# Expert routing in a two-block transformer kernel: 112 candidate sums in place of 256, and the last gate block copied beside the others

## The chip, the core and the metric

The kernel runs on one core of a Trainium2 chip. The metric is the device time of one execution in microseconds (us); a lower time is better. TensorE (PE) multiplies matrices, VectorE (DVE) and ScalarE (ACT) work elementwise, GpSimd (POOL) and SyncE (SP) issue transfers here. Each engine takes its instructions in the order in which the program was built, and a framework places that order with a model of its own when the kernel is built.

## The reference

The program computes two transformer blocks for 512 tokens of 1024 features. The change lies in the last part, a layer of 16384 experts (128 x 128 key pairs) in which every token is sent to 16 experts for each of 8 heads:

```python
q = (hc @ w_query).reshape(PEER_CHUNK, PEER_HEADS, PEER_KEY_DIM)
s1 = jnp.einsum('chk,nk->chn', q[..., :PEER_HALF_DIM], keys_1)
s2 = jnp.einsum('chk,nk->chn', q[..., PEER_HALF_DIM:], keys_2)
v1, i1 = lax.top_k(s1, 16)
v2, i2 = lax.top_k(s2, 16)
cand = (v1[..., :, None] + v2[..., None, :]).reshape(PEER_CHUNK, PEER_HEADS, -1)
cand_idx = (i1[..., :, None] * N_KEYS + i2[..., None, :]).reshape(...)
top_s, pos = lax.top_k(cand, 16)
experts = jnp.take_along_axis(cand_idx, pos, axis=-1)
gate = jax.nn.softmax(top_s)
act = jax.nn.gelu(jnp.einsum('chkd,cd->chk', jnp.take(expert_u, experts, axis=0), hc))
out = jnp.einsum('chkd,chk->cd', jnp.take(expert_v, experts, axis=0), gate * act)
```

Of the 256 sums of two sorted lists of 16, the pair (i, j), counted from zero, has (i+1)(j+1)-1 sums that are no smaller, so it can be among the best 16 only if (i+1)(j+1) is at most 16.

## The kernel before

The first 384 tokens meet all experts: `eu` holds 128 rows of weights (L1080, `run_ahead`), each one product of 24 matmuls with 384 columns on PE, then gelu on ScalarE, then a store to `spill` in memory. The last 128 tokens meet their own experts alone, whose rows are gathered by index on GpSimd's queue (L1156, `gather`), multiplied with the token and summed on VectorE (L1162, `gather_dot`; L1168, `gather_sum`).

The layer has these stages. **Routing** (L1187, `route`): eight rounds, one for each head. A round has two products of 24 matmuls with 512 columns for the query, the scores against 128 keys, `top16` (L1178) on VectorE for four token tiles and two halves, then the 256 sums `cand` (L1240) and `top16` over them for four token tiles; for token tile 3 `chosen` (L1198) turns positions into the expert numbers that the gathers of the next round use. Beside it each round runs nine experts of U and, from the second round on, 13 gathered rows. **Gates**: `chosen` for the 8 heads of the other tiles and the softmax. **Spreading** (L1272, `spread`): gates become a dense table [i2, i1, token] in blocks of 32 tokens; the first 11 blocks go through `gstage` to `gdram` in memory, the 12th stays on the chip as `glast`. **Last stage** (in `peer`): for each of 128 experts the stored activations `pact` (for the last 15, `kept`) are multiplied with the gates (L1123 for 11 blocks out of `gtile`, which is loaded for four experts at a time, L1124 for the 12th out of `glast`), split in a high and a low part (`pwh`, `pwl`), the row of V is loaded and split (`vh`, `vl`), and PE adds 24 matmuls into eight banks.

Every weight is split in two: ScalarE casts the high part (`split`, L190), VectorE subtracts the low part (L191, `wlo`), and PE's third matmul of a group needs it. The split weights have two buffers, so ScalarE's cast waits until PE has finished the product before. A shared pool `row` of five buffers holds the rows of U, of V and the gathered rows.

What sets the order: `later` (L164) gives U's matmuls a lower priority; everything else is taken by the framework in its modelled order of readiness. VectorE carries U's `wlo`, the gathered rows, and `top16` in one queue.

Of the kernel before, what the change touches and what calls it, by code (L numbers as in the profile page):

```python
# [33 lines left out]
# ---------------------------------------------------------------- host layout  # L34
# [116 lines left out]
class Builder:  # L151
# [12 lines left out]
    # the block's instructions give way to what is traced up to n instructions later  # L164
# [11 lines left out]
    # banks of the accumulator memory: six by number, two for the large products  # L176
# [6 lines left out]
    # the banks of the large products in turn: the two, and the given others while they are free  # L183
# [4 lines left out]
    # src -> hi + lo, both exact in float32r  # L188
# [13 lines left out]
    # n more buffers for the weights, or none  # L202
# [5 lines left out]
    # one [128, n] block of (x @ w).T; w in dram [128, kc, 128], x as hi / lo [128, kc, 512]  # L208
# [18 lines left out]
    # the same for several w, side by side: step blocks of x for each in turn  # L227
# [15 lines left out]
    # (ss / n + eps) ** -0.5 on a small tile  # L243
# [7 lines left out]
    # row vector over all partitions: out[p, t] = r[t % 128, t // 128]  # L251
# [6 lines left out]
    # sums of squares over the features: all blocks but the last are added up; over the partitions, token-major  # L258
# [13 lines left out]
    # 1 / rms over all partitions  # L272
# [9 lines left out]
    # h = rmsnorm(x) * sw + sh, split into hi / lo  # L282
# [15 lines left out]
    # x[m] += gate[m] * (w applied to the hi / lo source), sums of squares of the new x  # L298
# [10 lines left out]
    # 128 features of one section of silu(c) @ ada_w + ada_b, feature-major  # L309
# [19 lines left out]
    # the tiles still to do of the given sections, n at a time, behind more urgent work  # L329
# [17 lines left out]
    # sigmoid through exp  # L347
# [40 lines left out]
    # ------------------------------------------------------------ first block  # L388
    def block1(self):
        A, V, x = self.A, self.V, self.x  # L390
        with ExitStack() as st1:
# [7 lines left out]
            with ExitStack() as st2:  # L399
# [12 lines left out]
                # scale and shift of feature block k, and weights ahead of their first use  # L412
# [79 lines left out]
    # token-major part of the projection: ga, gbeta, ng, v_slc, v_win  # L492
    def proj_small(self, hi, lo):
# [7 lines left out]
        class Small:  # L501
            # the weights of the next feature blocks
# [43 lines left out]
    # depthwise causal convolution and silu of one block of the projection  # L546
# [47 lines left out]
    # decay rates, beta and the cumulated decays, token-major [128, head, token tile]  # L594
# [37 lines left out]
    # what of one head needs its keys alone: decays, the triangular inverse, w  # L632
    def gdn_inv(self, h):
# [7 lines left out]
        # f = beta / |k|^2, rn = |k|  # L641
# [26 lines left out]
        # X = (I + strictly upper Bm)^-1 by blocks of doubling size; Tm = X.T  # L668
# [27 lines left out]
        # k e^gc ; k f e^(gl - gc)  # L696
# [11 lines left out]
    # the rest of one head that does not need the state  # L708
# [17 lines left out]
    # scan over the chunks, the four heads together; output norm and gate  # L726
# [32 lines left out]
    def gdn_out(self):  # L759
# [3 lines left out]
        # rmsnorm(o) * w * silu(z); the missing |q| and dk^-0.5 go into its eps  # L763
# [15 lines left out]
    # keys and values of the three attentions; the norm weights of q go into the keys  # L779
# [58 lines left out]
    # the three attentions of one token tile; the output takes the place of q  # L838
    def nsa(self, kp, t, last):
# [7 lines left out]
        # compressed keys, four heads at once  # L847
# [90 lines left out]
    # ----------------------------------------------------------- second block  # L938
    def mixer2(self):
# [7 lines left out]
        with ExitStack() as st:  # L947
# [59 lines left out]
            # per-token sums over the 512 channels  # L1007
# [34 lines left out]
            self.update(A["wo2"], KD, mh, ml, self.mod(1, 2))  # L1042

    # The tokens up to ND meet every expert: gelu(U h), times a gate that is zero for the experts not chosen, times V.
    # The last 128 tokens meet their own experts, whose rows are gathered.
    def peer(self):
        A, V, C, x = self.A, self.V, self.C, self.x
        sw = self.scaled(1, 4, "n22")
# [281 lines left out]
```

## Time and profile before

| | |
|---|---|
| runs of the kernel before | 2490.15, 2495.16, 2498.87 us (median 2495.16) |
| the profiled execution | span 2508.0 us, 35062 instructions |
| PE busy | 2396.5 us (96%) |
| weight loads (PEld) busy | 2161.5 us (86%) |
| VectorE busy | 1848.0 us (74%) |
| ScalarE busy | 1071.4 us (43%) |
| GpSimd busy | 367.0 us (15%) |
| DMA | 509.39 MB, 203 GB/s on average |

The page gives no other time for the profiled execution than its span; it is 12.8 us above the median of the runs shown. Shares are averages over stages, so each stage is read by itself: the routing stage runs from 1157 to 1609 us of the span, gates to 1682, spreading to 1954, the last stage to 2491.

### The profile page before, as it was taken

Reading aid. Unit: us, or ns where it says so; the run is one execution under the profiler, and the core shown is the slowest. Engines: PE = TensorE matmul, PEld = TensorE weight load, DVE = VectorE, ACT = ScalarE, POOL = GpSimd, SP = SyncE. Lnnn points to the kernel's source line nnn. Section 1 sums busy time; section 2 is a strip of 40 time slices with the busy share of each in tenths; the row PEclk is TensorE's granted clock in tenths of the full one; section 3 lists DMA queues with packets and bytes.
Section 4 is the critical chain, followed back from the end, with each engine's and each line's share of the span. In section 5 each row is a group of like instructions: output and inputs, shape, how many; then the busy total and the mean of one; then the engine's idle time right before and its main releaser. Section 6 shows DMA issues by size and latency. Waiting matters only on the chain. (4 is left out here: it accounts for less than half of the span.)

```text
span 2508.0 us, 35062 instructions
## 1 busy us (share of the span) xinstructions
PE 2396.5 (96%) x12749; PEld 2161.5 (86%) x12749; DVE 1848.0 (74%) x3826; ACT 1071.4 (43%) x1751; POOL 367.0 (15%) x284
## 2 busy tenths in 40 slices
PE   8999999899999999999889998999998999999998
PEld 7788787678878777878888888999898999999997
DVE  6764634778874499657778888999886878887774
ACT  4534623343432233334222232459998433333332
POOL 0000000000000000000222222123210333334420
PEclk9999888899999999999999999999999999999998
DMA  7332102465554222243777776669885999999981
GB/s 277 126 124 68 43 9 84 165 199 190 190 182 138 78 97 90 70 151 101 241 245 253 256 231 229 220 221 323 317 294 201 326 335 344 336 348 311 347 304 59
DMA packets 197933, 509.39 MB, mean 203 GB/s; under 512 B 20352, under 2 KB 93312, under 8 KB 195840
## 3 DMA queue, kind: packets, MB, share of 16 engines
q1 hardware_dynamic: 160896, 372.92, 43.7%
q0 software_dynamic: 36864, 134.23, 15.6%
q8 instruction: 100, 1.64, 0.3%
q14 instruction: 73, 0.60, 0.1%
HBM read 459.71 MB, written 47.38 MB: 202 GB/s over the span
## 5 line engine op out<-in xcount | busy, mean ns | idle before, releaser
L162 PE MATMUL acc<-hi,wlo 128*128 128x384 f32 (+1 forms) x1488 | 544.5, 366 | 41.3 <-DVE wlo L191 40.9
L162 PE MATMUL acc<-hi,whi 128*128 128x384 f32 (+1 forms) x1488 | 541.2, 364 | 2.4 <-ACT whi L190 1.2
L162 PE MATMUL acc<-lo,whi 128*128 128x384 f32 (+1 forms) x1488 | 537.3, 361 | 0.0
L190 ACT CAST whi<-raw 128x1024 fp32r<-128x1024 f32 (+2 forms) x168 | 167.5, 999 | 443.8 <-PE p L162 234.7
L162 PEld LDWEIGHTS acc<-hi,wlo 128*128 128x128 f32 x1488 | 283.7, 191 | 77.1 <-DVE wlo L191 56.1
L162 PEld LDWEIGHTS acc<-hi,whi 128*128 128x128 f32 x1488 | 284.1, 191 | 23.9 <-ACT whi L190 2.1
L162 PEld LDWEIGHTS acc<-lo,whi 128*128 128x128 f32 x1488 | 283.9, 191 | 20.2 <-issue 1.0
L191 DVE TENSOR_TENSOR wlo<-raw,whi 128x1024 fp32r<-128x1024 f32 (+2 forms) x168 | 194.3, 1157 | 104.3 <-ACT whi L190 101.9
L190 ACT CAST whi<-row 128x1024 fp32r<-128x1024 f32 x128 | 135.1, 1055 | 307.8 <-PE acc L162 286.5
L1158 POOL DMA_INDIRECT row<-in_ev_dram,eidx x128 | 199.2, 1556 | 431.7 <-DVE vl L191 251.9
L162 PE MATMUL p<-pwl,vh 128*128 128x384 f32 x768 | 257.7, 336 | 0.9 <-DVE pwl L191 0.9
L162 PE MATMUL p<-pwh,vh 128*128 128x384 f32 x768 | 254.4, 335 | 2.6 <-ACT pwh L190 2.6
L162 PE MATMUL p<-pwh,vl 128*128 128x384 f32 x768 | 252.5, 336 | 0.0
L1158 POOL DMA_INDIRECT row<-in_er_dram,eidx x128 | 148.2, 1158 | 501.4 <-DVE row L1165 167.1
L1175 DVE SCALAR_TENSOR_TENSOR pN<-row,dots,pN 128x1024 f32<-128x1024 f32 x127 | 162.7, 1281 | 79.4 <-DMA row<-in_ev_dram,eidx 79.2
L1165 DVE SCALAR_TENSOR_TENSOR row<-row,hN 128x1024 f32<-128x1024 f32 x128 | 155.8, 1220 | 67.4 <-DMA row<-in_er_dram,eidx 66.9
L162 PE MATMUL p<-hi,whi 128*128 128x512 f32 x432 | 171.9, 404 | 8.2 <-ACT hi L292 6.4
L191 DVE TENSOR_TENSOR wlo<-row,whi 128x1024 fp32r<-128x1024 f32 x128 | 155.9, 1218 | 31.4 <-ACT whi L190 30.7
L191 DVE TENSOR_TENSOR vl<-row,vh 128x1024 fp32r<-128x1024 f32 x128 | 155.8, 1219 | 29.9 <-ACT vh L190 29.9
L190 ACT CAST vh<-row 128x1024 fp32r<-128x1024 f32 x128 | 133.8, 1051 | 97.3 <-DMA row<-in_ev_dram 51.7
L162 PE MATMUL p<-hi,wlo 128*128 128x512 f32 x432 | 173.8, 403 | 1.3 <-DVE wlo L191 1.3
L162 PE MATMUL p<-lo,whi 128*128 128x512 f32 x432 | 173.3, 401 | 1.7 <-DVE lo L293 1.7
(500 smaller groups left out, 4579.6 us busy)
## 6 DMA issues: line engine op xcount, KB each, us to landing
row<-in_eu_dram SPq DMA_DIRECT2D x128, 512.0 KB
row<-in_ev_dram SPq DMA_DIRECT2D x128, 512.0 KB
araw<-in_ada_dram SPq DMA_DIRECT2D x64, 512.0 KB
raw<-in_up_dram SPq DMA_DIRECT2D x44, 512.0 KB
gdram<-gstage SPq DMA_DIRECT2D x11, 2048.0 KB
gtile<-gdram SPq DMA_DIRECT2D x31, 704.0 KB
spill<-pact SPq DMA_DIRECT2D x113, 192.0 KB
pact<-spill SPq DMA_DIRECT2D x113, 192.0 KB
```

The costliest lines, as they stand in the source:

```text
L162: self.T.matmul(out, lhsT, rhs, start=start, stop=stop)
L190: self.C.copy(hi, src)
L191: self.V.tensor_tensor(lo, src, hi.bitcast(F32), ALU.subtract)
L1158: self.G.indirect_dma_start(out=u, out_offset=None, in_=self.A[src], in_offset=bass.IndirectOffsetOnAxis(ap=self.eidx[:, s:s + 1], axis=0))
L1165: self.V.scalar_tensor_tensor(u, u, 1.0, self.hN, ALU.mult, ALU.mult, accum_out=self.dots[:, s:s + 1])
L1175: self.V.scalar_tensor_tensor(self.pN, v, w, self.pN, ALU.mult, ALU.add)
```

## The change

Two edits, apart from removed comments.

**Sums.** A region of 112 sums takes the place of the 256: for the first four keys of the first half all 16 of the second, for the other twelve the first four of the second half (64 + 48). All pairs with (i+1)(j+1) at most 16 lie in it. The sums are made for token tile 3 and for tiles 0 to 2 together, in two pieces each, and `top16` goes over 112 columns. Since the position in this layout no longer has the first key in its upper bits, `chosen` gets three more operations that turn it into the position of the 256 layout.

```diff
-            V.tensor_scalar(ab[:, 0], px, 4, None, ALU.logical_shift_right)
-            V.tensor_scalar(ab[:, 1], px, 15, None, ALU.bitwise_and)
+            wide = rp.tile([P, n, 16], U32, name=f"wide{n}", bufs=1)
+            V.tensor_scalar(wide, px, 124, None, ALU.bitwise_and)
+            V.tensor_scalar(wide, wide, 64, 3, ALU.max, ALU.mult)
+            V.scalar_tensor_tensor(wide, wide, 192, px, ALU.subtract, ALU.add)
+            V.tensor_scalar(ab[:, 0], wide, 4, None, ALU.logical_shift_right)
+            V.tensor_scalar(ab[:, 1], wide, 15, None, ALU.bitwise_and)
...
+            cands = {}
+            for t0, n in ((3, 1), (0, 3)):
+                cand = rp.tile([P, n, NC], F32, name=f"cand{n}", bufs=2)
+                for i0, i1, nj in ((0, 4, 16), (4, 16, 4)):
+                    b4 = [P, n, i1 - i0, nj]
+                    o = cand[:, :, 0:64] if i0 == 0 else cand[:, :, 64:NC]
...
+                    V.tensor_tensor(o, a, b, ALU.add)
+                cands.update({t0 + i: cand[:, i, :] for i in range(n)})
             for t in (3, 0, 1, 2):
-                cand = rp.tile([P, 16, 16], F32, name="cand", bufs=2)
-                b3 = [P, 16, 16]
-                V.tensor_tensor(cand, v_[:, t, h, 0, :].unsqueeze(2).to_broadcast(b3),
-                                v_[:, t, h, 1, :].unsqueeze(1).to_broadcast(b3), ALU.add)
-                self.top16(cand.rearrange("p a b -> p (a b)"), ts[:, t, h, :], px[:, t, h, :])
+                self.top16(cands[t], ts[:, t, h, :], px[:, t, h, :])
```

**Gates of the last 32 tokens.** `gtile` gets a 12th block; ScalarE copies it from `glast` for four experts at a time, and one multiplication with 384 columns takes the place of two (352 and 32).

```diff
-                            gt = wk.tile([P, NB - 1, GA, TB], F32, name="gtile", bufs=2)[:, :, :n, :]
+                            gt = wk.tile([P, NB, GA, TB], F32, name="gtile", bufs=2)[:, :, :n, :]
...
-                        self.dma(gt, gd[:, :, e:e + n, :].rearrange("b p a t -> p b a t"))
+                        self.dma(gt[:, :NB - 1], gd[:, :, e:e + n, :].rearrange("b p a t -> p b a t"))
+                        C.copy(gt[:, NB - 1], gl[:, e:e + n, :])
...
-                    V.tensor_tensor(a3[:, :NB - 1, :], a3[:, :NB - 1, :], gt[:, :, e - e0, :], ALU.mult)
-                    V.tensor_tensor(a3[:, NB - 1, :], a3[:, NB - 1, :], gl[:, e, :], ALU.mult)
+                    V.tensor_tensor(a3, a3, gt[:, :, e - e0, :], ALU.mult)
```

PE's order is the same up to the end of the routing stage; the order of VectorE changes from the first round on. VectorE in the later part of a round, before (`wlo` is the low part of a weight of U, `row,dots` a gathered row, MAX, MAX_INDEX and MATCH_REPLACE are the steps of `top16`, `px` the positions found):

```order
L191 TENSOR_TENSOR wlo<-row,whi 128x1024
L1180 MAX ts<-cand 128x8
L1181 MAX_INDEX px<-ts,cand 128x8
L1165 SCALAR_TENSOR_TENSOR row,dots<-row,hN 128x1024
L1181 MAX_INDEX px<-ts,cand 128x8
L1182 MATCH_REPLACE cand<-ts,cand 128x256
L191 TENSOR_TENSOR wlo<-row,whi 128x1024
L1165 SCALAR_TENSOR_TENSOR row,dots<-row,hN 128x1024
L1182 MATCH_REPLACE cand<-ts,cand 128x256
L1183 MAX ts<-cand 128x8
L191 TENSOR_TENSOR wlo<-row,whi 128x1024
```

The same place on VectorE after:

```order
L191 TENSOR_TENSOR wlo<-row,whi 128x1024
L1181 MAX_INDEX px<-ts,cand_10487 128x8
L1181 MAX_INDEX px<-ts,cand_10490 128x8 x3
L1165 SCALAR_TENSOR_TENSOR row,dots<-row,hN 128x1024
L1182 MATCH_REPLACE cand_10487<-ts,cand_10487 128x112
L1182 MATCH_REPLACE cand_10490<-ts,cand_10490 128x112 x3
L191 TENSOR_TENSOR wlo<-row,whi 128x1024
L1165 SCALAR_TENSOR_TENSOR row,dots<-row,hN 128x1024
L1183 MAX ts<-cand_10487 128x8
L1183 MAX ts<-cand_10490 128x8 x3
L191 TENSOR_TENSOR wlo<-row,whi 128x1024
```

All four tiles are now searched together between two low parts, where before two were under way at a time.

ScalarE in the last stage, once it runs evenly, after (`pwh` is the high part of the gated activations, `vh` that of a row of V); before, the same casts alternate with no copy among them:

```order
L190 CAST vh<-row 128x1024
L1117 COPY gtile<-glast 128x128
L190 CAST pwh<-pact 128x384
L190 CAST vh<-row 128x1024
L190 CAST pwh<-pact 128x384
L190 CAST vh<-row 128x1024
L190 CAST pwh<-pact 128x384
L190 CAST vh<-row 128x1024
L190 CAST pwh<-pact 128x384
L190 CAST vh<-row 128x1024
L1117 COPY gtile<-glast 128x128
```

One copy stands in ScalarE's queue for every four experts.

VectorE where the last stage begins, before (`hN` holds the gates of the first two experts, `pN` is the sum of the gathered rows of V); the multiplications of the fifteen `kept` activations follow one another, of which three are shown:

```order
L1123 TENSOR_TENSOR pact<-pact,hN 128x352 x2
L1175 SCALAR_TENSOR_TENSOR pN<-row,dots,pN 128x1024
L1124 TENSOR_TENSOR pact<-pact,glast 128x32 x4
L1124 TENSOR_TENSOR kept_15430<-kept_15430,glast 128x32
L1124 TENSOR_TENSOR kept_15526<-kept_15526,glast 128x32
L1124 TENSOR_TENSOR kept_15604<-kept_15604,glast 128x32
```

And after:

```order
L1124 TENSOR_TENSOR pact<-pact,hN 128x384 x2
L1175 SCALAR_TENSOR_TENSOR pN<-row,dots,pN 128x1024
L191 TENSOR_TENSOR pwl<-pact,pwh 128x384
L191 TENSOR_TENSOR vl<-row,vh 128x1024
L191 TENSOR_TENSOR pwl<-pact,pwh 128x384
L191 TENSOR_TENSOR vl<-row,vh 128x1024
```

The nineteen small multiplications in front of the first low parts are gone; PE has 41 matmuls of U left behind its last product of the spreading stage, where it had 5.

## Rows read from the trace of the kernel before

**Rows 1.** Busy time by stage; columns: window, length, then each engine, clock, DMA.

```profile
1157.33:1608.56 451.23, 415.64 (x2212) 389.66 (x2210) 374.99 (x1166) 137.01 (x195) 101.10 (x91) 0.98 0.71 235
...
1681.69:1953.54 271.85, 254.54 (x1678) 247.27 (x1678) 222.92 (x609) 259.60 (x559) 57.20 (x48) 0.99 0.79 278
1953.54:2490.93 537.39, 536.44 (x3080) 535.65 (x3080) 419.49 (x624) 193.46 (x261) 176.68 (x108) 0.99 0.88 310
```

**Rows 2.** The same view of the eight runs of expert products between queries.

```profile
1162.26:1195.96 33.70, 33.70 (x194) 33.70 (x193) 27.43 (x99) 11.01 (x17) 3.99 (x3) 1.00 0.47 155
...
1273.94:1318.23 44.29, 37.57 (x196) 36.29 (x195) 35.98 (x116) 11.37 (x17) 11.84 (x11) 0.92 0.79 255
...
sum 325.47, PE 291.39 PEld 281.59 DVE 275.75 ACT 95.68 POOL 75.41; mean PE 36.42 PEld 35.20 DVE 34.47 ACT 11.96 POOL 9.43
```

**Rows 3.** Waits in the routing stage, of PE and VectorE: total us, times, longest.

```profile
PE acc L162 <- DVE wlo L191: 35.4, 26, 4.4
...
DVE row L1165 <- DMA row<-in_er_dram,eidx: 64.8, 49, 5.0
```

**Rows 4.** VectorE in order of time, head 5, 256 sums: start us, us, instruction.

```profile
1437.33 0.74 DVE L1183 MAX8 ts<-cand 128x8 f32<-128x256 f32 x2
1437.99 0.41 DVE L1211 TENSOR_TENSOR eq<-abf,ca 128x256 f32<-128x256 f32 x1
1438.31 0.08 DVE L1184 MATCH_VALUE_LOAD px<-ts,cand 128x8 f32 x1
...
1438.72 0.07 DVE L1184 MATCH_VALUE_LOAD px<-ts,cand 128x8 f32 x1
```

**Rows 5.** The same view, searches of 128 scores.

```profile
1398.44 0.85 DVE L1180 MAX8 tv<-rsc 128x8 f32<-128x128 f32 x4
1399.21 0.07 DVE L1184 MATCH_VALUE_LOAD tix<-tv,rsc 128x8 f32 x1
...
1399.47 0.07 DVE L1184 MATCH_VALUE_LOAD tix<-tv,rsc 128x8 f32 x1
```

**Rows 6.** The same view, two dependent operations on 16 columns.

```profile
1443.79 0.17 DVE L1245 SCALAR_TENSOR_TENSOR ch<-ch 128x16 f32<-128x16 f32 x1
1443.99 0.17 DVE L1246 CAST eidx<-ch 128x16 int32<-128x16 f32 x1
```

**Rows 7.** Waits of PE from 16 us into rounds 1 and 6 on.

```profile
PE acc L162 <- DVE wlo L191: 2.5, 2, 1.3
...
PE acc L162 <- DVE wlo L191: 5.3, 3, 3.7
```

**Rows 8.** VectorE in order of time, the longest stall for a gathered row.

```profile
1304.37 1.22 DVE L1165 SCALAR_TENSOR_TENSOR row<-row,hN 128x1024 f32<-128x1024 f32 x1 [4.96 <-DMA row<-in_er_dram,eidx]
```

**Rows 9.** VectorE in order of time, last stage, one expert of V.

```profile
2305.33 0.52 DVE L1123 TENSOR_TENSOR pact<-pact,gtile 128x352 f32<-128x352 f32 x1
2305.77 0.19 DVE L1124 TENSOR_TENSOR pact<-pact,glast 128x32 f32<-128x32 f32 x1
2305.87 1.22 DVE L191 TENSOR_TENSOR vl<-row,vh 128x1024 fp32r<-128x1024 f32 x1
```

**Rows 10.** PE in order of time where the last stage begins.

```profile
1953.54 1.31 PE L162 MATMUL p<-pwh,vh 128*128 128x384 f32 x6 [2.65 <-ACT pwh L190]
...
1956.44 0.69 PE L162 MATMUL p<-pwl,vh 128*128 128x384 f32 x1 [0.94 <-DVE pwl L191]
```

**Rows 11.** ScalarE casts of gated activations, the whole program: busy us, mean ns.

```profile
L190 ACT CAST pwh<-pact 128x384 fp32r<-128x384 f32 x113 | 58.0, 514 | 226.0 <-issue 135.0 <-PE acc L162 78.3 <-DVE pwl L191 4.7
```

**Rows 12.** ScalarE, VectorE and PE, last stage, where a row of V lands late.

```profile
2308.73 1.05 ACT L190 CAST vh<-row 128x1024 fp32r<-128x1024 f32 x1 [5.20 <-DMA row<-in_ev_dram]
...
2309.94 1.22 DVE L191 TENSOR_TENSOR vl<-row,vh 128x1024 fp32r<-128x1024 f32 x1
...
2311.13 0.33 PE L162 MATMUL p<-pwh,vh 128*128 128x384 f32 x1
```

**Rows 13.** VectorE in the spreading stage: a stall for a gathered row of V.

```profile
1894.92 1.29 DVE L1175 SCALAR_TENSOR_TENSOR pN<-row,dots,pN 128x1024 f32<-128x1024 f32 x1 [9.52 <-DMA row<-in_ev_dram,eidx]
```

More of the change, by code (lines that the diff above doesn't have):

```diff
@@ L1112, in peer @@
                         if e:
-                            gt = wk.tile([P, NB - 1, GA, TB], F32, name="gtile", bufs=2)[:, :, :n, :]
+                            gt = wk.tile([P, NB, GA, TB], F32, name="gtile", bufs=2)[:, :, :n, :]
                         else:
-                            gt = self.hN[:, :(NB - 1) * n * TB].rearrange("p (b a t) -> p b a t", b=NB - 1, a=n)
-                        self.dma(gt, gd[:, :, e:e + n, :].rearrange("b p a t -> p b a t"))
+                            gt = self.hN[:, :NB * n * TB].rearrange("p (b a t) -> p b a t", b=NB, a=n)
+                        self.dma(gt[:, :NB - 1], gd[:, :, e:e + n, :].rearrange("b p a t -> p b a t"))
+                        C.copy(gt[:, NB - 1], gl[:, e:e + n, :])
                     if e < KEPT:
@@ L1195, in route @@
         self.gi = self.gs_ = 0
+        NC = 112
         def chosen(px, ix, n, out=None):
@@ L1236, in route @@
                     self.top16(sc[:, t, :], v_[:, t, h, s, :], ix[:, t, h, s, :])
-            for t in (3, 0, 1, 2):
-                cand = rp.tile([P, 16, 16], F32, name="cand", bufs=2)
-                b3 = [P, 16, 16]
-                V.tensor_tensor(cand, v_[:, t, h, 0, :].unsqueeze(2).to_broadcast(b3),
-                                v_[:, t, h, 1, :].unsqueeze(1).to_broadcast(b3), ALU.add)
-                self.top16(cand.rearrange("p a b -> p (a b)"), ts[:, t, h, :], px[:, t, h, :])
+            cands = {}
[4 more added lines that the diff above has]
+                    o = cand[:, :, 0:64] if i0 == 0 else cand[:, :, 64:NC]
+                    o = o.rearrange("p t (i j) -> p t i j", j=nj)
+                    a = v_[:, t0:t0 + n, h, 0, i0:i1].unsqueeze(3).to_broadcast(b4)
+                    b = v_[:, t0:t0 + n, h, 1, 0:nj].unsqueeze(2).to_broadcast(b4)
+                    if n == 1:
+                        o, a, b = (v.squeeze(1) if hasattr(v, "squeeze") else v[:, 0] for v in (o, a, b))
+                    V.tensor_tensor(o, a, b, ALU.add)
+                cands.update({t0 + i: cand[:, i, :] for i in range(n)})
+            for t in (3, 0, 1, 2):
+                self.top16(cands[t], ts[:, t, h, :], px[:, t, h, :])
                 if t == 3:
```

## Prediction

> **What bounds the kernel now.** I read the busy time by stage first, then the same view of pieces of one stage, then the waits, then single stretches in order of time. In the last stage PE is busy for 536.4 of 537.4 us [rows 1]: 3080 matmuls, 174.5 ns each, 4.19 us for the 24 of one expert. Nothing that VectorE saves there can shorten it. In the routing stage PE is busy for 415.6 of 451.2 us and VectorE for 375.0 [rows 1], so neither is saturated, and the reader is to see why in the runs of expert products that lie between the queries of two heads [rows 2]. In the first run no rows are gathered yet, and 191 matmuls take 33.70 us at full clock, 176.4 ns each. All eight runs hold 191 + 6 x 193 + 219 = 1568 such matmuls, which would be 276.7 us at that rate; they take 325.47 us. So 48.8 us are lost, all in runs two to eight. The third is the worst: 44.29 us for 193 matmuls (34.0 at the full rate), with a mean clock of 0.92, so part of it ran at the lower of the two levels after a long wait. The waits say who is late: PE stood 35.4 us, 26 times, for `wlo`, the low part of a weight of U on VectorE, and VectorE itself stood 64.8 us, 49 times, for gathered rows [rows 3]. VectorE is therefore late partly by its work and partly by transfers, and the question of this change is what a shorter VectorE queue does to a stage with both.
>
> **The searches.** Head 5 shows the spacing of the steps on 256 sums [rows 4]: two MAX8 from 1437.33 to 1437.99 are 0.33 each, a FIND_INDEX8 with the load in front of it 1438.72 - 1438.31 = 0.41. A search is two MAX8, two FIND_INDEX8 and one MATCH_REPLACE8, which I take like FIND_INDEX8: 0.66 + 1.23 = 1.89 us. On 128 scores [rows 5] MAX8 is (1399.21 - 1398.44) / 4 = 0.19 and FIND_INDEX8 0.26, a search 0.38 + 0.78 = 1.16. The 128 columns cost 0.73, so 144 fewer save 0.82 us, and four tiles 3.3 us per head.
>
> **The sums.** Four sums of 256 at the spacing of MAX8 are 1.32 us per head. By the same slope (1.1 ns a column on 0.05) the new pieces of 48, 64, 144 and 192 columns are 0.10, 0.12, 0.21 and 0.26, in all 0.69. That saves 0.6; the bound on the bad side, for broadcasts in four dimensions that run slower, is no saving.
>
> **The three operations more in `chosen`.** They depend on each other. Two dependent operations on 16 columns start 0.20 us apart [rows 6]; the bounds are 0.08, the length of a value load in [rows 4], and 0.20. I take 0.20, since each reads what the one before wrote: 0.6 us per head. Net 3.3 + 0.6 - 0.6 = 3.3 us per head, 26 us in eight. The three calls for all heads at once add nine operations on 128 columns, each under the 0.41 of a step on 256 [rows 4], at most 3.7 us behind the routing stage, where PE has products of U in stock; I take 1 us.
>
> **What of it reaches the end.** The first round has no loss to recover, so at most 7 x 3.3 = 23 us. Below that the saving must meet a wait. The searches over sums begin some 16 us into a run; from there to the end of the run PE waits between 2.5 and 5.3 us in each of rounds 1 to 6 (the first and the last of six answers stand in [rows 7]; they are 2.5, 4.6, 3.5, 3.7, 3.5 and 5.3), 23.1 us together. In two of them the long wait, 4.4 and 3.7 us, follows a stall of VectorE for a gathered row, the worse one of 4.96 us [rows 8]; shorter searches don't bring that row sooner. That leaves 15 us of waits that sit behind VectorE's own work. Up to 3.3 us of work less per round against waits of 2.5 on average, some of which move on to the next gathered row: I take 12 us, from bounds of 0 (the gathered rows take all) and 23.
>
> **The gates of the last 32 tokens.** For one expert the two multiplications start 0.44 us apart, and the second is followed after 0.10 [rows 9]; with 384 columns instead of 352 I expect 0.48 in place of 0.54. That is VectorE's time in a stage in which PE is never idle [rows 1]: worth nothing, covered by PE, and 8 us if that cover were gone. ScalarE gets 32 copies of at most 128 columns, each under the 0.51 us of a cast of 384 [rows 11], 16 us at most, in a stage in which it is busy for 193.5 of 537.4 us [rows 1]. At the beginning of the stage PE stood 2.65 us for the first `pwh` and 0.94 for the first `pwl` [rows 10], with nineteen small multiplications in VectorE's queue between. In the changed order they are gone and 41 products of U, some 7 us, cover the end of spreading instead of 5. But ScalarE must still take the gelu of the last expert, then cast `pwh` and `vh`, before PE goes on. I take a gain of 1 us, from bounds of 4 lost and 4 gained.
>
> **Spreading** keeps its work, but its order moves. Before, a gathered row of V held VectorE for 9.52 us [rows 13] and with it the one-hot tables that PE needs. Such a stall can vanish or come twice; I take zero, within 6 us either way.
>
> Sum: 12 - 1 + 1 = 12 us. The profiled span of 2508.0 us would become 2496; against the median of the runs, 2495.2, it is **2483 us**. What a measurement of this kernel can tell from no change is about 0.3%, 7.5 us.
>
> **Rivals.**
>
> *The gathered rows take the saving.* Five `row` buffers serve weights of U and gathered rows; VectorE reaches the next gathered row sooner and waits longer for it, so the 64.8 us of [rows 3] grow by what the searches lose. For it: in rounds with gathers VectorE stands still somewhere in every one. Against it: 15 us of PE's waits sit behind VectorE's own work. It gives 0 to 4 us, about 2493. The Trainium skill has a rule that points this way (Perfetto Trace Analysis, Optimization Strategy): the same gap repeating on the engine that should be saturated can mean that there are too few buffers for the next tile. By that rule all of PE's waits are a matter of the five buffers and the time stays; the trace bears it out in the two long waits above, and not in the others.
>
> *The saving comes through whole.* Waits of over 3 us put PE's clock down to its lower level afterwards (the 0.92 of [rows 2]); if most fall away, the clock comes back as well, and the stall of [rows 13] may go with the new order. 23 us, some 4 of clock or stall, less 1: about 2469.
>
> *The copies hold the casts up: slower.* A copy into `gtile` may not start before VectorE has read the last activation of the tile two before, and the next `pwh` and `vh` stand behind it on ScalarE; on VectorE that read is queued behind gathered rows of V. While PE has a lead of several experts this costs nothing. From about 2280 to 2430 us the lead is gone: a row of V lands 5.20 us late, its low part runs from 2309.94 to 2311.16, and PE begins that expert at 2311.13 [rows 12]. There are (2430 - 2280) / 4.19 = 36 experts and nine copies in this stretch. If each holds the casts for one expert's share of VectorE, 419.5 / 128 = 3.3 us [rows 1], that is 30 us lost against 12 gained: about 2513. It decides from the point where a copy comes free later than the next row of V lands. Against it: VectorE needs 3.3 us of the 4.19, and activations are gated well ahead of rows of V. The Trainium skill (TensorE: Matmul & The Clock Gate, Architectural detail: the array is 16x 32x32) has ScalarE and VectorE take their queues strictly in order, which this rival needs; the trace agrees, with everything behind the stall of [rows 13] waiting 9.52 us.
>
> *The new order loses elsewhere what routing gains.* A second stall like that of [rows 13], about 10 us with its slow clock, gives 2495.
>
> **How the numbers follow.** Forecast, 2476 to 2489: 0.55. Gathered rows take it, 2491 to 2497: 0.22. Whole, 2463 to 2475: 0.13. Copies, 2500 to 2515: 0.06. Lost elsewhere, 2492 to 2500: 0.04. The range that leaves out the copies and the better part of the whole saving is 2467 to 2499. Faster by over 0.3% (under 2487.7) are nine tenths of the forecast and the whole saving, 0.62; slower (over 2502.6) the copies and a little of the last case, 0.07; the rest, 0.31, is within.
>
> **What would show it.** Right: in the runs of [rows 2] the sum falls from 325 to about 313 us and PE's wait for `wlo` from 35 to about 23; searches on 112 columns last some 0.15 us less a step than on 256; VectorE's busy time in routing falls by some 26 us; the last stage still takes 24 matmuls in 4.19 us per expert. Wrong: VectorE's wait for gathered rows grows by as much as its work falls (first rival); PE waits for `vl` or `pwh` in the last third of the last stage (the copies); the spreading stage differs from 272 us by more than 6.

## The result and the profile after

The changed kernel takes **2512.6 us** (median of 10 runs), the kernel before 2498.4 us on the same chip (median of 10): a ratio of 1.0068, with a 95% interval of 1.0043 to 1.0092. It is slower by 0.7%, some 17 us by the ratio and 14 by the medians. The forecast was 2483 us, faster; the time lies above the range of 2467 to 2499.

The profiled executions have spans of 2515.6 and 2508.0 us. The part of the program ahead of routing is the same in both and happened to run 10 us shorter after: the first expert product behind the first scores starts at 1147.23 instead of 1157.33 us, and over all the kernels of this text between 1142 and 1157. So the changed part by itself is 18.5 us longer, and I compare it in two pieces. The first is routing, gates and spreading up to the first product with V, the second the last stage. Busy time by stage, first the kernel before (its last stage stands in [rows 1]):

```profile
1157.33:1953.54 796.21, 740.27 (x4282) 705.00 (x4280) 667.96 (x1849) 428.08 (x801) 170.67 (x148) 0.98 0.73 246
```

and the changed kernel:

```profile
1147.23:1954.63 807.40, 746.28 (x4282) 711.17 (x4280) 643.55 (x1873) 428.65 (x802) 175.55 (x148) 0.98 0.71 242
1954.63:2499.32 544.69, 537.51 (x3079) 535.70 (x3080) 412.02 (x503) 201.94 (x293) 178.72 (x108) 0.99 0.87 306
```

Behind the length stand the busy times of PE, of the weight loads and, third, of VectorE: 24.4 us of work less in the first piece, as forecast, and yet the piece is 11.2 us longer, 7.4 of them in routing and gates and 3.8 in spreading. The last stage is 7.3 us longer with nearly the same work for PE.

The searches cost what the forecast said. VectorE in order of time in the changed kernel, one head:

```profile
1407.79 0.80 DVE L1180 MAX8 ts<-cand 128x8 f32<-128x112 f32 x4
1408.51 1.21 DVE L191 TENSOR_TENSOR wlo<-row,whi 128x1024 fp32r<-128x1024 f32 x1
...
1409.70 0.27 DVE L1181 FIND_INDEX8 px<-ts,cand 128x8 uint32<-128x112 f32 x1
...
1409.95 0.27 DVE L1181 FIND_INDEX8 px<-ts,cand 128x8 uint32<-128x112 f32 x1
...
1424.05 0.17 DVE L1206 SCALAR_TENSOR_TENSOR wide<-wide,px 128x16 uint32<-128x16 uint32 x1
1424.25 0.17 DVE L1207 TENSOR_SCALAR ab<-wide 128x16 uint32<-128x16 uint32 x1
```

Four MAX8 fit between 1407.79 and 1408.51, 0.18 us each, where [rows 4] had 0.33; one FIND_INDEX8 starts 0.25 behind the other, where it was 0.41; a dependent operation on 16 columns takes 0.20, as in [rows 6].

The gain is missing in the eight runs of expert products (same view as [rows 2]):

```profile
1152.17:1185.87 33.70, 33.70 (x194) 33.70 (x193) 25.04 (x103) 11.03 (x17) 4.71 (x4) 1.00 0.52 173
1206.90:1250.85 43.95, 37.18 (x197) 35.89 (x196) 35.61 (x135) 11.38 (x17) 10.81 (x10) 0.92 0.71 237
...
sum 325.27, PE 286.68 PEld 279.54 DVE 271.62 ACT 94.06 POOL 74.82; mean PE 35.83 PEld 34.94 DVE 33.95 ACT 11.76 POOL 9.35
```

The sum is 325.27 us, as before, though the runs now hold 26 matmuls fewer (1542 instead of 1568). The waits show what took the place of the work. Routing and gates, total, times and longest; the kernel before:

```profile
DVE row L1165 <- DMA row<-in_er_dram,eidx: 66.9, 51, 5.0
...
PE acc L162 <- DVE wlo L191: 37.4, 29, 4.4
```

and the changed kernel:

```profile
DVE row L1165 <- DMA row<-in_er_dram,eidx: 106.3, 49, 5.6
...
PE acc L162 <- DVE wlo L191: 45.3, 24, 4.1
```

VectorE waits 39 us more for gathered rows, in as many waits: more than the 24 us of work that it lost. PE's wait for `wlo` grew by 8 us with it, where the forecast had it fall by 12.

The last stage loses 4.5 of its 7.3 us within its first 72 matmuls (view of [rows 10], with VectorE beside it):

```profile
1954.63 0.44 PE L162 MATMUL p<-pwh,vh 128*128 128x384 f32 x1 [1.92 <-ACT vh L190]
1959.24 0.69 PE L162 MATMUL p<-pwl,vh 128*128 128x384 f32 x1 [4.16 <-DVE pwl L191]
...
1957.43 1.28 DVE L1175 SCALAR_TENSOR_TENSOR pN<-row,dots,pN 128x1024 f32<-128x1024 f32 x1 [3.95 <-DMA row<-in_ev_dram,eidx]
1958.63 0.55 DVE L191 TENSOR_TENSOR pwl<-pact,pwh 128x384 fp32r<-128x384 f32 x1
```

In front of the first `pwl` VectorE's queue holds a sum with a gathered row of V, and the row lands 3.95 us late. PE waits 4.16 us, where it waited 0.94 before, and waits another 1.05 us for a later `pwl`. After the first wait it runs below full speed (busy by window, mean clock 0.59):

```profile
1959.24:1966.00 6.76, 6.76 (x24) 6.76 (x25) 3.85 (x6) 1.56 (x3) 1.01 (x1) 0.59 0.94 278
```

The kernel before did so too at this place, with a mean clock of 0.62 from 1953 to 1962 us, so the difference lies in the waits. The rest of the 7.3 us comes late in the stage, around two short waits for `vl` (1.18 us at 2298 and 0.57 at 2354).

### The profile page after: what moved, and what is told of

It is laid out like the page before. It is cut to its first block, busy times and chain, and to the rows that moved or that the text cites. A ratio compares the mean times of both kernels' runs of the same rounds, so it can differ in the third digit from the quotient of the medians.

```text
span 2515.6 us, 34954 instructions
## 1 busy us (share of the span) xinstructions
PE 2394.7 (95%) x12749; PEld 2162.6 (86%) x12749; DVE 1816.2 (72%) x3731; ACT 1079.9 (43%) x1784; POOL 374.8 (15%) x284
## 5 line engine op out<-in xcount | busy, mean ns | idle before, releaser
L162 PE MATMUL p<-pwh,vl 128*128 128x384 f32 x768 | 243.5, 335 | 2.0 <-DVE vl L191 2.0
L1158 POOL DMA_INDIRECT row<-in_er_dram,eidx x128 | 154.3, 1205 | 520.6 <-DVE row L1165 122.2
```

The source lines that it names most:

```text
L162: self.T.matmul(out, lhsT, rhs, start=start, stop=stop)
L1158: self.G.indirect_dma_start(out=u, out_offset=None, in_=self.A[src], in_offset=bass.IndirectOffsetOnAxis(ap=self.eidx[:, s:s + 1], axis=0))
```

## Experiments

The table has all kernels in order. The pieces are the two from above, in us of one execution; kernels whose instructions stand in the same order up to the last stage differ by up to 11 us in the first piece (f2 and g2), so one difference of a few us there proves little. "Own" stands for buffers of their own for the gathered rows and "pause" for a later start of the sums with gathered rows of V; both are explained below. The last column is explained with the copies.

| kernel | ratio to before, 95% | routing to spreading | last stage | issues of gathered V rows waiting for `pN` |
|---|---|---|---|---|
| before | 1 | 796 | 537 | 6 |
| changed | 1.0068 (1.0043 to 1.0092) | 807 | 545 | 0 |
| e1, sums alone | 1.0095 (1.0068 to 1.0122) | 804 | 548 | 0 |
| e2, copy alone | 1.0100 (1.0066 to 1.0134) | 797 | 560 | 223 |
| e3, changed, 6 own buffers | 0.9947 (0.9925 to 0.9969) | 765 | 544 | 12 |
| e4, before, 6 own buffers | 1.0018 (0.9994 to 1.0041) | 784 | 549 | 0 |
| e5, changed, pause | 1.0054 (1.0028 to 1.0079) | 810 | 534 | 0 |
| e6, changed, 6 own, pause | 0.9877 (0.9832 to 0.9921) | 765 | 535 | 29 |
| e7, e6 without copy | 0.9879 (0.9837 to 0.9922) | 765 | 536 | 30 |
| e8, e2 with three `gtile` | 1.0041 (1.0013 to 1.0068) | 798 | 556 | 139 |
| e9, e2 copied by VectorE | 1.0107 (1.0080 to 1.0135) | 798 | 554 | 230 |
| e10, before, 6 own, pause | 0.9984 (0.9964 to 1.0004) | 785 | 538 | 0 |
| e11, e1 with long searches | 1.0088 (1.0056 to 1.0121) | 809 | 534 | 0 |
| e12, e7 with 3 own | 0.9945 (0.9919 to 0.9971) | 780 | 535 | 0 |
| f1, e1, sums per tile | 1.0168 (1.0145 to 1.0190) | 832 | 542 | 0 |
| f2, before, chain alone | 1.0261 (1.0235 to 1.0287) | 811 | 584 | 152 |
| f3, e2 with pause | 1.0129 (1.0100 to 1.0158) | 805 | 568 | 232 |
| f4, e7 with 10 own | 0.9926 (0.9902 to 0.9950) | 765 | 541 | 0 |
| g1, e2, five `pwh`, `pwl` | 1.0099 (1.0068 to 1.0131) | 797 | 556 | 203 |
| g2, f2, five `pwh`, `pwl` | 1.0209 (1.0163 to 1.0254) | 799 | 577 | 217 |

### Each edit alone

e1 takes the changed kernel and puts the two multiplications per expert back; e2 takes the kernel before and makes only the copy. Each has one half of the change's diff.

> The 112 sums alone; the last gate block is multiplied from glast as before. Its routing, gates and spreading have the changed kernel's order on every engine; the last stage that of the kernel before. Theory A (both edits lose): the traces put +7.4 us on routing and gates and +3.8 on spreading, so about 11 us over the kernel before, and a last stage of 537 us. Theory B (the copies lose everything, the traces' difference in routing is chance): within 3 us of the kernel before, routing and gates 528 us. Forecast's theory (searches gain): 11 us under it.

> The copy of the last gate block alone; the 256 sums stay. Order as in the kernel before up to the first product of the last stage. Theory A: routing, gates and spreading as before (529 and 268 us), the last stage about 545 us, so 7 us over the kernel before. Theory B: 17 us over it. If the late start of the last stage in the changed kernel belongs to its new queue from spreading on and not to the copies: within 2 us of the kernel before.

Both lose, each at least as much as the two together: 1.0095 and 1.0100 against 1.0068, with intervals that overlap. e1 has the order of the changed kernel up to the last stage and 804 us there, near theory A's 807, but its last stage took 548 us, where theory A had 537. e2 loses nothing in its 797 us and 23 us in the last stage, three times what theory A expected and more than theory B's 17:

```profile
1950.95:2511.15 560.20, 543.93 (x3079) 536.68 (x3080) 409.09 (x500) 192.58 (x288) 151.19 (x107) 0.99 0.86 295
```

That is e2's last stage: VectorE has 10 us less to do than in [rows 1], PE stands idle for 16. The two losses don't add up (1.95% in all against 0.7%), so at least one of the losses is not a price of the edit itself.

### Buffers of their own for the gathered rows

```diff
     def gather(self, src, s):
-        u = self.row()
+        u = self.grow()
...
+        self.grow = lambda: rp.tile([P, D], F32, name="grow", bufs=6)
```

During routing `grow` has six buffers beside the five of `row`; from the spreading stage on it is `row` again.

> The changed kernel, but rows gathered during routing have six buffers of their own instead of sharing the five of row. Theory of the buffers: the gathers are issued earlier, VectorE's wait for gathered rows in routing (106 us there and in the gates) falls under 40, the runs of expert products fall from 326 to about 305 us and the kernel gains some 15 to 25 us over the changed one, and it gains more than the kernel before does by the same buffers. Theory of the order (the products with gathered rows stand too early in VectorE's queue, whatever the buffers): the wait stays above 80 us and the time within 5 us of the changed kernel's.

> The kernel before with the same six buffers of their own for rows gathered during routing. Theory of the buffers: VectorE's wait for gathered rows falls from 67 us to under 40, the gain is 5 to 15 us over the kernel before, and this kernel is slower than the changed one with the same buffers by about 10 us, the saving that the forecast expected. Theory of the order: within 5 us of the kernel before.

Busy time by stage, the changed kernel with own buffers, then the kernel before with them:

```profile
1151.71:1917.00 765.29, 727.69 (x4283) 699.50 (x4281) 644.51 (x1873) 428.27 (x802) 178.86 (x148) 0.99 0.72 256
```

```profile
1146.67:1930.67 784.00, 734.51 (x4282) 703.64 (x4280) 665.74 (x1858) 427.86 (x801) 183.27 (x148) 0.99 0.72 249
```

VectorE's work differs by 21.2 us and the piece by 18.7: nearly all of the saving comes through. The waits of the changed kernel with own buffers, in routing and gates:

```profile
DVE grow L1166 <- DMA grow<-in_er_dram,eidx: 28.8, 23, 4.5
...
PE acc L162 <- DVE wlo L191: 12.1, 16, 1.4
```

106 us of waiting have become 29, PE's wait for `wlo` 45 has become 12. The issues' waits for a product that has not yet given its buffer back fall from 92 us in the changed kernel to 16, and from 148 in the kernel before to 14 in e4. The cause can also be read from the time between the issue of a gather and the start of its product on VectorE, over the first 91 gathers: with the shared buffers its median is 5.7 us before and 5.8 after, with a minimum of 4.2 and 4.1, and nine in ten products start within 7.1 us. VectorE stood waiting in front of 49 of the 91 in the kernel before, so it takes most rows about as soon as they land. With six own buffers the median is 10.4 us: most rows lie ready. That `row` then serves U alone is not what helps, for rows of U were not late before: ScalarE waited for one once, 4.8 us, in routing and gates of the kernel before, and never in those of the changed kernel. The planner makes a new order here too, so e3 by itself does not separate buffers from order; three, six and ten buffers, further down, do it better.

With own buffers the changed kernel gains 0.5% over the kernel before, 1.2 points more than without the buffers. The kernel before gains 12 us in the first piece as well, and gives 11 back in the last stage, where PE now waits 8.3 us for the first `pwl`, so its time stays (1.0018). The changed kernel with own buffers has the same wait there, 8.4 us.

### The pause at the start of the last stage

Here the sums with gathered rows of V that stand in the loop of the last stage begin with its fifth expert:

```diff
-                    self.gather_sum(1)
+                    if e >= 4:
+                        self.gather_sum(1)
```

> The changed kernel, but the sums with gathered rows of V pause for the first four experts of the last stage, so none stands in VectorE's queue ahead of the first pwl. Theory of the queue: PE's wait of 4.16 us for the first pwl falls under 1 us and the slow clock after it goes with it, the last stage takes about 538 us, and the kernel is 6 to 8 us faster than the changed one (about 1.004 of the kernel before). Theory of the supply (rows of V come late for everything at that point): PE waits as long for vl or vh, time within 3 us of the changed kernel.

> The changed kernel with six buffers of their own for the rows gathered during routing, and with the pause of the gathered sums at the start of the last stage. If the two causes add up: the 8.4 us wait for the first pwl goes, the last stage falls from 544.5 to about 537 us, and the ratio to the kernel before is about 0.991. If the wait only moves on to the first rows of V: 0.994, as without the pause.

> The same without the copy of the last gate block (two multiplications per expert, the last block out of glast). If the copies cost something in this form: 3 to 15 us faster than the kernel with them, ratio under 0.99. If they cost only where VectorE lags behind, as with 256 sums: within 3 us of it.

In e5 the first `pwl` is ready in time (PE in order of time, and the stage):

```profile
1958.76 0.44 PE L162 MATMUL p<-pwh,vh 128*128 128x384 f32 x1 [1.92 <-ACT vh L190]
1959.04 0.34 PE L162 MATMUL p<-pwl,vh 128*128 128x384 f32 x1
```

```profile
1958.76:2493.00 534.24, 533.80 (x3079) 533.21 (x3080) 413.92 (x505) 203.03 (x293) 192.91 (x112) 1.00 0.90 314
```

The stage is 10 us shorter at once. The timed runs of e5 alone do not settle it: 1.0054 fits the expectation, but its interval overlaps that of the changed kernel. With own buffers the step is clear: 0.9947 becomes 0.9877; the last stage falls from 544 to 535 us. e7 shows that the copies cost nothing here (0.9879 without them): two stages of 535 and 536 us, PE busy throughout:

```profile
1911.94:2447.80 535.86, 535.68 (x3080) 534.77 (x3080) 421.02 (x614) 194.66 (x261) 186.19 (x112) 1.00 0.90 313
```

e6 and e7 beat both kernels, at 2469.6 and 2466.0 us beside 2499.3 for the kernel before.

> The kernel before (256 sums, no copy) with six buffers of their own for rows gathered during routing and the pause of the gathered sums at the start of the last stage; against the same with 112 sums (ratio 0.988) it shows what the shorter searches are worth when no gathered row waits for a buffer. If they are worth what VectorE saves (19 us in the traces of the two kernels with own buffers): ratio 0.994 to 0.997. If the buffers and the pause alone carry the gain: 0.988 to 0.990.

e10 has everything of e7 but the 112 sums: 0.9984 against 0.9879, which is 26 us by the ratios and 23 by the two traces (1323.7 us for both pieces against 1300.7). That is nearly the whole saving of the searches, once gathered rows seldom wait for a buffer. Buffers and pause without the shorter searches gain next to nothing in the timed runs (0.2%, with an interval from 0 to 0.4).

> 112 sums without the copy, the pause of the gathered sums, and three instead of six buffers of their own for rows gathered in routing. A gathered row takes 4 to 6 us from issue to its product, and 13 rows come in a round of about 58 us, so three buffers should be enough if only the sharing with the rows of U delayed the issues: within 5 us of the kernel with six (ratio 0.988 to 0.990). If VectorE takes rows in bursts that three buffers do not cover: ratio 0.992 or more and a wait for gathered rows above 60 us.

> 112 sums without the copy, the pause, and ten instead of six buffers of their own for rows gathered in routing (ratio 0.988 with six, 0.9945 with three). If six still hold issues back: a wait for gathered rows under 20 us in place of 28, and 3 to 6 us faster than with six. If the rest of the wait is the transfer itself: within 3 us of six.

Three own buffers give half of it (0.9945, first piece 780 us): the expectation that three would do was wrong. VectorE still waits 44.5 us for rows, whose issues wait 68.5 us for products that have not yet given their buffer back. Ten leave the first piece at 765 us and the wait for rows at 26, and bring 541 in the last stage instead of 536; six are enough. From shared buffers over three to six the wait goes from 106 to 44.5 and 28 us, the median from issue to product from 5.8 to 7.0 and 10.3, and the piece from 807 to 780 and 765.

### What loses the time of the sums

e11 puts the old length of the searches back (tiles of 256 columns, 144 of them filled once), f1 the old place of the sums (each tile's two pieces ahead of its own search), and f2 adds to the kernel before only the chain of three operations:

```diff
+            V.tensor_scalar(wide, px, 255, None, ALU.bitwise_and)
+            V.tensor_scalar(wide, wide, 0, 1, ALU.max, ALU.mult)
+            V.scalar_tensor_tensor(wide, wide, 0, px, ALU.subtract, ALU.max)
```

> The 112 sums alone (ratio 1.0095), but the searches go over 256 columns, 144 of them filled once with a very small number, so that the layout of the sums and the three operations more in chosen stay and the searches take as long as before. The order on TensorE is nearly that of the kernel before. If the shorter searches lose the time, by the queue order and the gathered rows that they bring: routing back to 428 to 433 us, ratio 0.999 to 1.004. If the new layout or the longer chain in chosen loses it: routing 435 us or more, ratio 1.008 or more.

> The 112 sums alone, made for each token tile directly ahead of its own search, in two pieces (eight small operations a head instead of four), as the 256 sums were placed before. With the sums of tiles 0 to 2 made together the ratio was 1.0095, and 1.0088 with searches of the old length. If the joint sums in one block ahead of the searches lose it (VectorE meets the gathered rows in bursts): ratio 0.997 to 1.003 and VectorE's wait for gathered rows back from 100 to about 70 us. If the chain in chosen or any new order loses it: 1.007 to 1.011.

> The kernel before with three more dependent operations in chosen, which leave the position as it is; sums and searches are those of 256. They add 0.6 us per head to VectorE by the forecast's count. If the longer chain loses the time of the sums edit (it delays the expert numbers, and the planner moves the work around it): ratio 1.005 to 1.011. If not: 0.998 to 1.003.

The two stages of e11:

```profile
1147.37:1956.43 809.06, 747.90 (x4282) 714.37 (x4280) 670.83 (x1887) 427.95 (x801) 172.91 (x148) 0.97 0.73 242
1956.43:2490.93 534.50, 533.79 (x3079) 533.21 (x3080) 418.87 (x619) 192.63 (x261) 163.46 (x108) 1.00 0.89 311
```

VectorE has the old work again, 27 us more than in the changed kernel, and the first piece is as long: 809 us against 804, 807 and 810 in the three kernels with the changed order, short searches and shared buffers (e1, the changed kernel, e5). What moved instead is its wait for gathered rows in routing and gates, 26 us less than the 106.3 of the changed kernel:

```profile
DVE row L1165 <- DMA row<-in_er_dram,eidx: 80.3, 52, 4.5
```

So with shared buffers the length of the searches makes no difference to the piece that these runs can tell. The ratios of e11 and e1, 1.0088 and 1.0095, say less, for the last stages behind them differ (534 and 548 us). f1 makes the sums tile by tile and is the worst of the three (832 us, 117 us of waits for gathered rows), so undoing the joint sums does not bring the time back. f2 leaves sums and searches alone and loses 2.6% by three small operations, 0.6 us a head by the forecast's count, where 0.5 to 1.1% was the most expected:

```profile
1963.38:2547.30 583.92, 550.73 (x3079) 537.59 (x3080) 416.10 (x610) 187.57 (x258) 142.66 (x107) 0.99 0.83 282
```

Most of it is in a last stage that it does not touch, so it is no price of the three operations. What all of these kernels change is the order that the framework's planner makes. Which feature of the order in routing costs the 8 and 13 us of e1 and e11 (804 and 809 us against 796) stays open.

### What loses the time of the copy

In e2 ScalarE stands in front of the copies, as the rival on copies said (waits in the last stage, total, times, longest):

```profile
POOL row L1158 <- DVE pN L1175: 223.4, 76, 7.2
ACT vh L190 <- DMA row<-in_ev_dram: 157.9, 57, 7.5
ACT gtile L1117 <- DVE pact L1124: 112.2, 27, 7.5
```

In the changed kernel the third of these is 39.7 us. Four runs tried to take the loss away: a third `gtile`, VectorE as the copying engine, the pause, and a fifth buffer for `pwh` and `pwl` (which also went into f2):

```diff
-                            gt = wk.tile([P, NB, GA, TB], F32, name="gtile", bufs=2)[:, :, :n, :]
+                            gt = wk.tile([P, NB, GA, TB], F32, name="gtile", bufs=3)[:, :, :n, :]
...
-                        C.copy(gt[:, NB - 1], gl[:, e:e + n, :])
+                        V.tensor_copy(gt[:, NB - 1], gl[:, e:e + n, :])
...
-                    wh = wk.tile([P, ND], F32R, name="pwh", bufs=LAST + 1)
+                    wh = wk.tile([P, ND], F32R, name="pwh", bufs=LAST + 2)
```

> The copy of the last gate block alone, with 256 sums, and three buffers for gtile instead of two. Theory of the copy's wait (a copy holds ScalarE until VectorE has read the tile two before, and the casts queue behind it): ScalarE's 112 us of waits for gtile fall under 30, the last stage falls from 560 to about 540 us, and the kernel comes within 0.3% of the kernel before. Theory of the shorter slack elsewhere (order of casts, transfers): the last stage stays above 553 us and the ratio at 1.01.

> The copy of the last gate block alone, with 256 sums, but made by VectorE instead of ScalarE. The copy then follows VectorE's own last reading of the tile, so ScalarE has nothing to wait for. Theory of the queue (the copy's place in ScalarE's queue costs, not the copy): ScalarE's waits for gtile (112 us with the copy on ScalarE) are gone, the last stage falls from 560 to 538 to 545 us and the ratio to the kernel before from 1.010 to under 1.004. If the wider multiplication or the larger tile costs by itself: the last stage stays above 553 us, ratio 1.008 or more.

> The copy of the last gate block alone on ScalarE, with 256 sums, and the pause of the gathered sums for the first four experts of the last stage. With the copy alone the last stage took 560 us, and pwl was ready only about 1 us ahead of PE from the 25th expert on, against 11 us before. If the late start of the stage costs the lead and it is never won back: last stage 536 to 542 us, ratio under 1.003, as the pause brought 545 to 534 us in the changed kernel. If the order of the casts in the stage keeps the lead low: still over 550 us, ratio 1.007 or more.

> The copy of the last gate block alone (ratio 1.010), with five buffers for pwh and pwl instead of four. With four, vl of an expert stands ahead of its pwl in VectorE's queue for all experts of the last stage; in the kernel before pwl stands ahead of vl for 57 of 128 and just behind the vl before for another 49. With five, pwl stands level with or ahead of vl for all but five. If that order takes the lead of pwl: last stage 536 to 545 us, ratio 0.998 to 1.004. If the copy costs in another way: above 552 us, ratio 1.008 or more.

> The three operations more in chosen alone (ratio 1.026, last stage 584 us), with five buffers for pwh and pwl; the order of pwl and vl changes in the same way. If the order of the two low parts was the cause: last stage 536 to 550 us, ratio 1.003 to 1.012 (what is left is routing and gates, 10 us). If the longer chain costs in another way: above 570 us, ratio 1.02 or more.

None brought the stage under 554 us. The first two changes are e8's and e9's, the third, with the same for `pwl`, that of g1 and g2. With a third tile the planner issues each copy one tile earlier, right behind the reading that frees it, and ScalarE waits 95 us all the same. Its stage of 556 us is that of an execution of 2519.3 us, 10.5 above the median of its runs; the ratio of 1.0041 lets it seem that part of the loss was gone in the others. With VectorE copying, ScalarE has no such wait, and the stage still takes 554 us: **the copy's place in ScalarE's queue is not what makes the stage long**. Nor is the wider multiplication, which e9 keeps: e6 has it too, in a stage of 535 us. The pause leaves 568 us. Five buffers move PE's waits from `pwl` to `vl` (in g1 10.9 us in 8 waits for `vl`, where e2 had 16.2 in 15 for `pwl`) and the stage stays at 556 and 577 us, so the order of the two low parts is not it either.

After these runs I looked at the addresses that the planner gave to the `row` tiles when it built the kernels. In the last stage rows of V (V) and gathered rows of V (N) take turns, and the five buffers (0 to 4) go round in two ways; the kernel before, then e2:

```
V3 N0 V2 N4 V1 N3 V0 N2 V4 N1 V3 N0 V2 N4
V0 N2 V1 N4 V3 N2 V0 N4 V1 N2 V3 N4 V0 N2
```

Before, every buffer serves both in turn, so a row waits for the one five places back. In e2 the gathered rows keep two buffers to themselves through most of the stage, and each waits until the sum two gathered rows back is done. That is the first of the three waits above: 223 us of issues waiting for `pN`, where the kernel before has 6. In the kernel before the issues wait as long, but for `vl` (251.9 us), so in e2 the gathered rows hang on each other, with two under way at most. The split over all kernels is clean. The seven in which 60 to 89 gathered rows take the buffer of a gathered row (e2, e8, e9, f2, f3, g1, g2) have 139 to 232 us of such waits and last stages of 554 to 584 us. The other thirteen, with 5 to 19 such rows, have at most 30 us and stages of 534 to 549. It fits all twenty kernels and names a mechanism, but no run changes this assignment alone (one with separate buffers for the two kinds in the last stage would), so it is argued, not shown.

## Why the prediction was wrong

Term by term, the gain of 12 less 1 in routing and gates was a loss of 7.4 us, the zero for spreading a loss of 3.8, and the gain of 1 in the last stage a loss of 7.3.

**The prices were right.** Searches, sums and chain save 24.4 us of VectorE's work by the trace, where the steps gave 26 less 1. With own buffers and the pause they are worth 23 to 26 us of time (e7 against e10).

**The step that failed is "What of it reaches the end".** I sorted PE's 23 us of waits in the second half of the rounds into those behind a stall for a gathered row and 15 us "behind VectorE's own work", and let shorter work shrink the latter by 12. The sorting was by the wait that came last. But the gathered rows pace VectorE's whole queue: half of its products with them stand waiting for the row, 5.7 us after the issue in the median, and the issue itself waits for a buffer that VectorE gives back (148 us in 40 waits). Work taken out between two rows is waited away at the next row: 24 us of work went, and VectorE's wait for gathered rows grew by 39. The row that speaks for this stood in [rows 3], 49 waits in seven rounds, some seven a round; I read it as a share of the delay instead of as the rhythm of the queue. e11 is the nearest test, though the planner reorders there too: with shared buffers the old searches bring 27 us of work back, 26 us of the waits go, and the first piece stays. With own buffers the saving comes through, 18.7 us (e3 against e4) to 23 (e7 against e10).

**The lower bound was wrong too.** I took "the gathered rows take all" as the worst case, zero. The first rival had the mechanism right (waits grow as work falls), but I gave it 2493, not a loss. The rule of the Trainium skill beside it (Perfetto Trace Analysis, Optimization Strategy), that equal gaps repeating on the engine that should be busy can mean too few buffers, came true here: e3 changes the buffers and PE's wait for `wlo` falls from 45 to 12 us. The kernels with the old order take 796 to 805 us for the first piece (six executions, mean 798.7), those with the changed order 804 to 810 (three, mean 807.2): a loss of some 8 us that no operation explains. That it comes from the planner's order is likely, not shown.

**The start of the last stage** was put at a gain of 1, within 4 either way; the first 72 matmuls lost 4.5 and the stage 7. I looked for the cost in ScalarE's casts and counted the nineteen multiplications that vanish from VectorE's queue, and did not ask what else stood in front of the first `pwl`: the gathered sum, which the order on record shows there. The rival that the new order loses elsewhere was the nearest to this, but it looked for the loss in spreading. That the stage before was at its floor (537 us against 534 to 536 in the best kernels) meant that its order could only be lost. Of the change and the eighteen experiments, thirteen have last stages of over 540 us.

**The copies.** Their mechanism was real in e2 and in the changed kernel (112 and 40 us of ScalarE's waits), but it decided nothing: e9 takes the wait away and stays slow, e6 has the copies and is at the floor. The time of 2513 that this rival gave is near the measured one by chance: it had 30 us lost to copies against 12 gained, and neither happened.

**Spreading** kept within its 6 us: 271.3 us from its first product after (1683.32 to 1954.63), 267.5 before (1686.01 to 1953.54).

## What to carry to other kernels

Before pricing a cut on an engine that waits often for transfers, take the time from issue to use: when it is close to its minimum (here 5.7 us against 4.2), the transfers set the pace, and the buffers have to come first. Here buffers and pause alone gained 0.2%, the cut alone lost 1%, and all together gained 1.2%. Where a planner sets the order and the buffers, a stage that stands at its floor is a state to be protected: three operations more a head moved another stage by 47 us, so every edit has to be read in all stages.

## What was not expected of the hardware

A gathered row of 128 x 1024 took at least 4.0 us from its issue on GpSimd to the start of its product, whatever the buffers (the least of the first 91 lies between 4.0 and 5.1 in each of the twenty kernels). After the wait of 4.16 us at the start of the last stage the granted clock was at the lower of its two levels, 1.2 GHz, for most of the next 6.8 us (mean 0.59), and 24 matmuls took 6.76 us there instead of 4.19: the slow clock cost 2.6 us on top of the wait. In the kernel before the lower level came at the same place too, behind a wait of 2.65 us.
